# Four feed-forward stages: one 512-column product for a weight's high part in place of two of 256 columns, with the halves summed on VectorE

## The chip, the cores and the metric

The kernel runs on one core of one Trainium2 chip. The metric is the device time of one execution in microseconds (us), as the median of several runs; lower is better.

## The reference, cut to what matters

Two blocks are applied to one sequence of 256 positions with 1024 channels, all in float32. The first has a gated mixer, a SwiGLU feed-forward stage, a banded attention and another SwiGLU stage. The second has, twice, a mixer (convolution, block attention and gated linear attention) and a feed-forward stage with a causal convolution of three taps between the two matrix products. So there are four feed-forward stages (FFN), two without taps and two with:

```python
def _swiglu_ffn(x, g_norm, w_gate_up, w_down):
    h = _rms_norm(x, g_norm)
    gate, up = jnp.split(h @ w_gate_up, 2, axis=-1)
    return (jax.nn.silu(gate) * up) @ w_down
...
        u = causal_depthwise_conv(h @ ffn_w_up[l].astype(h.dtype), ffn_conv_w[l], ffn_conv_b[l])
        x = x + (jax.nn.silu(u[..., :D_FF]) * u[..., D_FF:]) @ ffn_w_down[l].astype(x.dtype)
```

The hidden width is 2816 in all four, which is 22 blocks of 128.

## The kernel before

**Split products.** TensorE multiplies in fp32r, a rounded float32. To keep float32 accuracy every operand is split into a high part, which is the value rounded to fp32r, and a low part, which is the remainder. A product of two split operands is three products on TensorE: high by high, high by low and low by high.

**The weight stream** (class `Stream`). SyncE loads weights in units of two tiles of 128x1024 into three `raw` buffers. ScalarE writes the high part of a tile (`_hi`, L105, "hi" below), and VectorE the low part (`_lo`, L116, "lo" below). `LOOK = 8` pairs of such tiles (`wh`, `wl`) are kept, so the split runs up to eight tiles ahead of TensorE, and `pump` issues the next hi and lo between other work. Four of the down weights of each FFN are split early into buffers of their own (`xh`, `xl`).

**An FFN stage** (`ffn`). The activations stand transposed in SBUF as `hT`, channels on partitions, 256 positions as columns, eight blocks `k` of 128 channels, in two tiles for high and low. The first two of the 22 blocks of the hidden width are computed in another layout (`mmA`). For each block `i` from 2 to 21, a "pair" below, `mmB2` computes the gate and the up projection with two weight tiles. `mmB` runs three products of 256 columns for each `k` (L350 to L352), eight `k`, so a pair is 48 products. They fill one PSUM bank with 256 columns of gate and 256 of up. `finish` makes the activation of the pair: Silu on ScalarE (L628), a multiplication on VectorE (L629), and the split into `ah` and `al` (`split2`, L232 on ScalarE and L233 on VectorE). In the two stages with taps it first applies them: bias and last tap on ScalarE (L617), the two other taps on VectorE (L622, four instructions), all reading PSUM.

Behind the pair, `down` (L374 to L376) multiplies the activation of three pairs ago by its down weight into four accumulators `acc` of 512 columns, 12 products of 512 columns for a pair: two halves `t` of 128 positions, two halves of the 1024 output channels, three products each. At the end of a stage the last activations are needed at once. `boundary` then adds the accumulators to the stream `x`, normalises it, and transposes it into the next `hT`, while `down` for the second half of the positions (`tail`) keeps TensorE at work.

**PSUM.** There are eight banks in one pool. Four hold `acc` during most of an FFN stage, and four are left for the pairs, of which each takes one.

**Order.** SyncE's queue is in program order. The order of the other engines' instructions is set when the program is built, by a scheduler that knows program order and its own costs.

Of the kernel before, what the change touches and what calls it, by code (L numbers as in the profile page):

```python
# [8 lines left out]
F32 = mybir.dt.float32  # L9
F32R = mybir.dt.float32r  # L10
U32 = mybir.dt.uint32
AF = mybir.ActivationFunctionType
# [3 lines left out]
P = 128  # L16
S = 256
D = 1024
KD = D // P
# [28 lines left out]
class Stream:  # L48
# [3 lines left out]
    def __init__(self, nc, raw_pool, pool, units):  # L52
        self.nc, self.raw_pool, self.pool = nc, raw_pool, pool
        self.units = units
        self.raw = {}
        self.split = {}
        self.index = []
        for u, (src, ext) in enumerate(units):
            for j, e in enumerate(ext):
                self.index.append((u, j, j == len(ext) - 1, e))  # L60
        self.next_dma = 0
        self.nh = 0
        self.nl = 0
        self.used = 0
        self.order = [[i for i, p in enumerate(self.index) if p[3] == e] for e in (False, True)]
        self.ext_pool = None
        self.ext_left = 0
        self.row_gain = {}
# [82 lines left out]
class Net:  # L151
    def __init__(self, ctx, tc, a, out, units):
        self.tc, self.nc, self.a, self.out = tc, tc.nc, a, out
        nc = self.nc
        en = ctx.enter_context
        self.cst = en(tc.tile_pool(name="cst", bufs=1))


        self.cst.tile([P, 32], F32, name="pad")
        self.raw_pool = en(tc.tile_pool(name="raw", bufs=RAW))  # L160
        self.wpool = en(tc.tile_pool(name="w", bufs=LOOK))
        self.hpool = en(tc.tile_pool(name="h", bufs=4))
        self.work = en(tc.tile_pool(name="work", bufs=2))
        self.small = en(tc.tile_pool(name="small", bufs=8))
        self.small.tile([P, 48], F32, tag="pad", name="pad", bufs=1)
        self.psum = en(tc.tile_pool(name="psum", bufs=8, space=bass.MemoryType.PSUM))
        en(tc.manual_schedule(engines={mybir.EngineType.SP}))
        self.ws = Stream(nc, self.raw_pool, self.wpool, units)
        self.x = [self.cst.tile([P, D], F32, name=f"x{t}") for t in range(2)]
        self.acc = None  # L170
        self.own = {}
# [13 lines left out]
    def mm(self, shape, name="mm"):  # L185
        return self.psum.tile(shape, F32, tag="mm", name=name, bufs=8)
# [37 lines left out]
        return y  # L224

    def new_hT(self):
        return tuple(
            self.hpool.tile([P, KD, S], F32R, tag="hT", name=n) for n in ("hTh", "hTl")
        )

    def split2(self, hi, lo, src):
        self.nc.scalar.activation(hi, src, AF.Copy)  # L232
# [111 lines left out]
    def mmB(self, out, hT, w):  # L344

        mm = self.nc.tensor.matmul
        vh = w[0].rearrange("p (k n) -> p k n", n=P)
        vl = w[1].rearrange("p (k n) -> p k n", n=P)
        for k in range(KD):
            mm(out, lhsT=vh[:, k, :], rhs=hT[0][:, k, :], start=(k == 0), stop=False)  # L350
            mm(out, lhsT=vh[:, k, :], rhs=hT[1][:, k, :], start=False, stop=False)  # L351
            mm(out, lhsT=vl[:, k, :], rhs=hT[0][:, k, :], start=False, stop=(k == KD - 1))  # L352

    def mmB2(self, hT, name="mm"):

        ids, ws = self.ws.take(2)
        ps = self.mm([P, 2, S], name)
        for j in range(2):
            self.mmB(ps[:, j, :], hT, ws[j])
        self.ws.release(ids)  # L360
        return ps
# [239 lines left out]
    def ffn(self, hT, fin, next_gains, conv=None, final=False):  # L601
        nc = self.nc
        with self.tc.tile_pool(name="ff", bufs=1) as pool:
            self.ws.ext(pool, DEFER)
            acts = {}

            def finish(i, ps):

                if conv is None:
                    g, u = ps[:, 0, :], ps[:, 1, :]  # L610
                else:
                    gu = pool.tile([P, 2, S], F32, tag="gu", name="gu", bufs=2)
                    ws3 = []
                    for j in range(2):
                        q = C_FCV + (conv * 44 + j * NPAIR + i) * 4
                        w = [self.prm[:, q + n : q + n + 1] for n in range(4)]
                        nc.scalar.activation(gu[:, j, :], ps[:, j, :], AF.Identity,  # L617
                                             bias=w[3], scale=w[2])
                        ws3.append(w)
                    for d in (1, 2):  # L620
                        for j in range(2):
                            nc.vector.scalar_tensor_tensor(  # L622
                                gu[:, j, d:], ps[:, j, : S - d], ws3[j][2 - d], gu[:, j, d:],
                                op0=ALU.mult, op1=ALU.add,
                            )
                    g, u = gu[:, 0, :], gu[:, 1, :]
                sg = pool.tile([P, S], F32, tag="sg", name="sg", bufs=2)
                nc.scalar.activation(sg, g, AF.Silu)  # L628
                nc.vector.tensor_mul(sg, sg, u)  # L629
                act = tuple(  # L630
                    pool.tile([P, S], F32R, tag=n, name=n, bufs=7) for n in ("ah", "al")
                )
                self.split2(act[0], act[1], sg)
                acts[i] = act

            ids, ws = self.ws.take(4)
            raws = []
            for t in range(2):
                ps = self.mm([P, 512])
                self.mmA(ps, hT, t, ws, 512, 2, fin if t == 0 else None)  # L640
                gr = self.work.tile([P, 512], F32, tag="hn", name="gr", bufs=2)
                nc.scalar.activation(gr[:, :256], ps[:, :256], AF.Copy)
                nc.vector.tensor_copy(gr[:, 256:], ps[:, 256:])
                raws.append(gr)
                self.ws.pump(2)
            self.ws.release(ids)
            self.ws.pump(2)
            held = []
            for i in range(2, NPAIR):
                ps = self.mmB2(hT)  # L650
                if i == 2:
                    for pr in range(2):
                        pt = self.mm([P, 2, S], "tr")
                        for t in range(2):
                            for j in range(2):
                                c = (j * 2 + pr) * P
                                nc.tensor.transpose(pt[:, j, t * P : (t + 1) * P],
                                                    raws[t][:, c : c + P], self.ident)
                        finish(pr, pt)
                if i < NPAIR - 1:  # L660
                    self.ws.pump(2)
                finish(i, ps)
                if i == 3:
                    self.new_acc()
                if i == 12:
                    gs = [self.gain(g) for g in next_gains]
                d = i - 3
                if d < 0:
                    continue
                ids, ws = self.ws.take(1, d >= NPAIR - DEFER)  # L670
                part = [(acts[d], ws[0])]
                self.down(0, part, d == 0, False)
                if d < NPAIR - DEFER:
                    self.down(1, part, d == 0, conv == 1 and d == NPAIR - DEFER - 1)
                    self.ws.release(ids)
                else:
                    held.append((ids, part[0]))
                if i < NPAIR - 1:
                    self.ws.pump(2)
            for ds in ((NPAIR - 3,), (NPAIR - 2, NPAIR - 1)):  # L680
                ids, ws = self.ws.take(len(ds), True)
                parts = [(acts[d], w) for d, w in zip(ds, ws)]
                self.down(0, parts, False, len(ds) == 2)
                held += [([i], p) for i, p in zip(ids, parts)]

            def tail(mid=None, cuts=(0, 512, 1024)):
                self.down(1, [p for _, p in held], conv == 1, True, mid, cuts)
                for ids, _ in held:
                    self.ws.release(ids)
                self.ws.ext(None, 0)  # L690

            if final:
                return self.boundary([gs[1]], tail, gs[0])
            if conv == 1:
                return gs, tail
            return self.boundary(gs, tail)
# [768 lines left out]
```

## Time and profile before

| what | value |
|---|---|
| median of 3 runs | 1251.49 us (1251.44 to 1251.61) |
| the profiled execution: time, span from first to last instruction | 1251.51 us, 1249.7 us |
| TensorE busy | 1239.1 us, 99% |
| VectorE busy, ScalarE busy | 847.9 us (68%), 666.2 us (53%) |
| granted clock of TensorE, mean | 0.999 of 2.4 GHz |

Durations in the trace are those of single instructions. Products on TensorE overlap one another, so what one costs is read from start to start and not from its duration. ScalarE's and VectorE's instructions overlap their neighbours by some 0.07 to 0.1 us. "PEld" is the loading of weights into the array, which goes on beside the products. A bracket at the end of a row of the timeline gives the idle time ahead of the instruction and what ended it.

### The profile page before, as it was taken

To read this page: it belongs to the slowest core of one execution; us is meant where nothing else is said; L and a number is where in the kernel's file an instruction comes from. 1 tells how busy PE (TensorE), PEld (TensorE's weight loads), DVE (VectorE), ACT (ScalarE), POOL (GpSimd) and SP (SyncE) were. 2 spreads that over 40 slices of the span, in tenths; PEclk is the share of its full clock that TensorE was granted. 3 is DMA by queue.
4 is the path that set the end of the run, shared out by engine and by line. 5 is a ranking of instruction groups with operands and counts; after the bars stand their busy time and mean duration, and the time that the engine had idled before them with its cause. 6 is when DMAs were issued, how large, how long until landed. Compare 5 with 4: busy or idle time off the path is not lost.

```text
span 1249.7 us, 20742 instructions
## 1 busy us (share of the span) xinstructions
PE 1239.1 (99%) x8440; PEld 1122.3 (90%) x8440; DVE 847.9 (68%) x1337; ACT 666.2 (53%) x1077; POOL 40.1 (3%) x95
## 2 busy tenths in 40 slices
PE   8999999999999999999999999999999999999997
PEld 7899899999888889999989878999998978999997
DVE  6676565555567756565568867777775977868764
ACT  7644454544456545454446556556553745656542
POOL 1100000000000000000010010000001011000000
PEclk9999999999999999999999999999999999999999
DMA  7754465665444435566524345456542415555710
GB/s 286 305 200 169 152 217 188 217 255 185 153 165 165 160 136 202 184 235 242 183 103 169 118 162 193 173 200 257 197 169 82 168 74 219 203 195 210 250 71 34
DMA packets 34836, 226.29 MB, mean 181 GB/s; under 512 B 4243, under 2 KB 4661, under 8 KB 9141
## 3 DMA queue, kind: packets, MB, share of 16 engines
q1 hardware_dynamic: 34596, 224.97, 49.2%
q8 instruction: 66, 1.08, 0.3%
q14 instruction: 30, 0.24, 0.1%
q10 hardware_dynamic: 144, 0.00, 0.0%
HBM read 223.91 MB, written 1.05 MB: 180 GB/s over the span
## 4 chain that ended last, share of the span: by engine, by line
PE 97%; DVE 1%; ACT 1%; DMA 0%; POOL 0%; issue 0%; POOLq 0%; ACTq 0%
PE mm L350 17%; PE mm L351 17%; PE mm L352 17%; PE mm L339 12%; PE acc L374 9%; PE acc L375 9%; PE acc L376 9%; PE tr L239 1%; PE sc L709 1%; PE mm L478 1%; PE pt L740 1%; PE sp L559 1%; PE po L798 1%; ACT sq L196 0%; PE po L1165 0%; PE dS L1053 0%
## 5 line engine op out<-in xcount | busy, mean ns | idle before, releaser
L116 DVE TENSOR_TENSOR wl<-raw,wh 128x1024 fp32r<-128x1024 f32 x378 | 458.4, 1223 | 253.2 <-ACT wh L105 250.4
L105 ACT ACTIVATE wh<-raw 128x1024 fp32r<-128x1024 f32 x378 | 394.7, 1055 | 321.6 <-PE mm L351 220.3
L350 PE MATMUL mm<-hTh,wh 128*128 128x256 f32 x1728 | 491.0, 284 | 0.0
L351 PE MATMUL mm<-hTl,wh 128*128 128x256 f32 x1728 | 489.0, 283 | 0.1
L352 PE MATMUL mm<-hTh,wl 128*128 128x256 f32 x1728 | 488.8, 283 | 0.0
L350 PEld LDWEIGHTS mm<-hTh,wh 128*128 128x128 f32 x1728 | 331.1, 192 | 8.4 <-issue 5.2
L351 PEld LDWEIGHTS mm<-hTl,wh 128*128 128x128 f32 x1728 | 331.2, 192 | 3.7 <-DVE hTl L233 0.5
L352 PEld LDWEIGHTS mm<-hTh,wl 128*128 128x128 f32 x1728 | 331.2, 192 | 0.0
L374 PE MATMUL acc<-wh,ah 128*128 128x512 f32 x320 | 126.0, 394 | 0.0
L375 PE MATMUL acc<-wl,ah 128*128 128x512 f32 x320 | 125.4, 392 | 0.0
L376 PE MATMUL acc<-wh,al 128*128 128x512 f32 x320 | 124.5, 389 | 0.0
L339 PE MATMUL mm<-wl,hTh 128*128 128x512 f32 (+1 forms) x240 | 90.2, 381 | 0.0
L339 PE MATMUL mm<-wh,hTh 128*128 128x512 f32 (+1 forms) x240 | 90.1, 381 | 0.0
L232 ACT ACTIVATE ah<-sg 128x256 fp32r<-128x256 f32 x88 | 36.3, 415 | 84.0 <-DVE sg L629 84.0
L622 DVE SCALAR_TENSOR_TENSOR gu<-mm,prm,gu 128x255 f32<-128x255 f32 (+1 forms) x160 | 66.5, 476 | 13.8 <-ACT gu L617 13.6
L376 PEld LDWEIGHTS acc<-wh,al 128*128 128x128 f32 x320 | 60.1, 188 | 13.2
L374 PEld LDWEIGHTS acc<-wh,ah 128*128 128x128 f32 x320 | 60.4, 189 | 10.8 <-issue 0.3
L375 PEld LDWEIGHTS acc<-wl,ah 128*128 128x128 f32 x320 | 60.4, 189 | 9.5
L339 PE MATMUL mm<-wh,hTl 128*128 128x512 f32 (+1 forms) x240 | 61.5, 384 | 0.0
L233 DVE TENSOR_TENSOR al<-sg,ah 128x256 fp32r<-128x256 f32 x88 | 37.1, 424 | 30.1 <-ACT ah L232 30.1
L339 PEld LDWEIGHTS mm<-wl,hTh 128*128 128x128 f32 x240 | 45.1, 188 | 9.3 <-issue 1.1
L339 PEld LDWEIGHTS mm<-wh,hTh 128*128 128x128 f32 x240 | 45.1, 188 | 9.0 <-issue 0.7
(217 smaller groups left out, 1252.0 us busy)
## 6 DMA issues: line engine op xcount, KB each, us to landing
raw<-in_w_ffn SPq DMA_DIRECT2D x66, 1024.0 KB, 4.8
raw<-in_w_up SPq DMA_DIRECT2D x66, 1024.0 KB, 5.0
raw<-in_w_mix SPq DMA_DIRECT2D x30, 1024.0 KB, 4.7
raw<-in_w_gmlp SPq DMA_DIRECT2D x22, 1024.0 KB, 4.8
raw<-in_w_att SPq DMA_DIRECT2D x16, 1024.0 KB, 4.8
raw<-in_w_gmlp SPq DMA_DIRECT2D x4, 512.0 KB, 6.3
bias<-in_rel SPq DMA_DIRECT2D x8, 256.0 KB, 3.9
x<-in_x SPq DMA_DIRECT2D x4, 256.0 KB, 5.4
```

Source lines behind the costliest of these rows:

```text
L105: self.nc.scalar.activation(hi, r, AF.Copy, scale=1.0 if g is None else g)
L116: self.nc.vector.tensor_sub(lo, r, hi.bitcast(F32))
L232: self.nc.scalar.activation(hi, src, AF.Copy)
L233: self.nc.vector.tensor_sub(lo, src, hi.bitcast(F32))
L339: mm(out, lhsT=hT[a][:, k, ts], rhs=view(b, k), start=(i == 0), stop=(i == 3 * KD - 1))
L350: mm(out, lhsT=vh[:, k, :], rhs=hT[0][:, k, :], start=(k == 0), stop=False)
L351: mm(out, lhsT=vh[:, k, :], rhs=hT[1][:, k, :], start=False, stop=False)
L352: mm(out, lhsT=vl[:, k, :], rhs=hT[0][:, k, :], start=False, stop=(k == KD - 1))
L374: mm(acc, lhsT=act[0][:, ts], rhs=w[0][:, c], start=(first and i == 0), stop=False)
L375: mm(acc, lhsT=act[0][:, ts], rhs=w[1][:, c], start=False, stop=False)
L376: mm(acc, lhsT=act[1][:, ts], rhs=w[0][:, c], start=False, stop=(last and i == n - 1))
L622: nc.vector.scalar_tensor_tensor(gu[:, j, d:], ps[:, j, : S - d], ws3[j][2 - d], gu[:, j, d:], op0=ALU.mult, op1=ALU.add,)
```

## The change

In `ffn` the high part of a weight tile now meets both parts of the activations in one product of 512 columns (`wide`), and its low part meets the high activations in one of 256 columns (`low`). For this the high and the low activations of a `k` lie side by side in one tile (`new_hT`). The wide product leaves high by high in the first 256 columns of a PSUM bank and high by low in the second 256, and the low product is added into the first half. So gate and up need a bank each, and `finish` has to add the two halves of each: ScalarE copies the second half out of PSUM and VectorE adds the first to it, into a tile `sum` in SBUF. What follows (Silu or the taps) reads `sum`. In the stages with taps, Silu is done in place. The other users of `mmB` are not changed.

```diff
     def new_hT(self):
-        return tuple(
-            self.hpool.tile([P, KD, S], F32R, tag="hT", name=n) for n in ("hTh", "hTl")
-        )
+        t = self.hpool.tile([P, KD, 2, S], F32R, tag="hT", name="hT")
+        return t[:, :, 0, :], t[:, :, 1, :], t
...
+    def mmB_wide(self, hT, w):
+        mm = self.nc.tensor.matmul
+        ps = self.mm([P, 2, S])
+        vh = w[0].rearrange("p (k n) -> p k n", n=P)
+        vl = w[1].rearrange("p (k n) -> p k n", n=P)
+        def wide(k):
+            mm(ps, lhsT=vh[:, k, :], rhs=hT[2][:, k], start=(k == 0), stop=(k == KD - 1))
+        def low(k):
+            mm(ps[:, 0, :], lhsT=vl[:, k, :], rhs=hT[0][:, k, :], start=False, stop=False)
+        for k in range(KD):
+            for f in (wide, low) if k < KD - 1 else (low, wide):
+                f(k)
+        return ps
...
             def finish(i, ps):
+                if isinstance(ps, list):
+                    raw = pool.tile([P, 2, S], F32, tag="sum", name="sum", bufs=2)
+                    for j in range(2):
+                        nc.scalar.activation(raw[:, j, :], ps[j][:, 1, :], AF.Copy)
+                    for j in range(2):
+                        nc.vector.tensor_add(raw[:, j, :], ps[j][:, 0, :], raw[:, j, :])
+                    ps = raw
...
-                sg = pool.tile([P, S], F32, tag="sg", name="sg", bufs=2)
+                if conv is None:
+                    sg = pool.tile([P, S], F32, tag="sg", name="sg", bufs=2)
+                else:
+                    sg = g
...
             for i in range(2, NPAIR):
-                ps = self.mmB2(hT)
+                if wide:
+                    ids, ws = self.ws.take(2)
+                    ps = [self.mmB_wide(hT, w) for w in ws]
+                    self.ws.release(ids)
+                else:
+                    ps = self.mmB2(hT)
```

## Rows read from the trace of the kernel before

**Rows 1.** The page, part 1: busy time, share of the span, instructions.
```profile
PE 1239.1 (99%) x8440; PEld 1122.3 (90%) x8440; DVE 847.9 (68%) x1337; ACT 666.2 (53%) x1077; POOL 40.1 (3%) x95
```

**Rows 2.** The page, part 4: the chain that ended last, by engine.
```profile
PE 97%; DVE 1%; ACT 1%; DMA 0%; POOL 0%; issue 0%; POOLq 0%; ACTq 0%
```

**Rows 3.** Groups of instructions: products of the changed loops and of others.
```profile
L350 PE MATMUL mm<-hTh,wh 128*128 128x256 f32 x1728 | 491.0, 284 | 0.0
```

**Rows 4.** The timeline of TensorE over one pair and its down products (start, duration).
```profile
799.48 0.28 PE L350 MATMUL mm<-hTh,wh 128*128 128x256 f32 x1
...
805.23 0.40 PE L374 MATMUL acc<-wh,ah 128*128 128x512 f32 x1
...
807.98 0.28 PE L350 MATMUL mm<-hTh,wh 128*128 128x256 f32 x1
```

**Rows 5.** The chain in order of time: start, length, what, count.
```profile
354.42 10.90 PE mm L339 x48
...
664.33 11.50 PE mm L339 x72
```

**Rows 6.** Groups by shape, and single lines (minimum/median/maximum in ns): 256-column work.
```profile
L642 ACT ACTIVATE gr<-mm x8: 364/371/380, 159.3 to 1067.4; 128x256 f32<-128x256 f32 x8
...
L629 DVE TENSOR_TENSOR sg<-sg,mm x40: 413/415/416, 176.4 to 635.9; 128x256 f32<-128x256 f32 x40
...
L617 ACT ACTIVATE gu<-mm,prm x80: 546/552/567, 778.4 to 1232.6; 128x256 f32<-128x256 f32 x80
...
L932 ACT ACTIVATE cy<-hpad,prm x4: 601/602/603, 661.3 to 966.3; 128x256 f32<-128x256 f32 x4
...
L622 DVE SCALAR_TENSOR_TENSOR gu<-mm,prm,gu 128x255 f32<-128x255 f32 x80 | 35.0, 477 | 13.8 <-ACT gu L617 13.6
...
L921 DVE SCALAR_TENSOR_TENSOR cy<-hpad,prm,cy 128x256 f32<-128x256 f32 x120 | 51.2, 478 | 1.6 <-ACT cy L932 1.3
```

**Rows 7.** The timeline of VectorE over one pair of a stage with taps.
```profile
899.91 1.23 DVE L116 TENSOR_TENSOR wl<-raw,wh 128x1024 fp32r<-128x1024 f32 x1 [1.41 <-ACT wh L105]
901.05 1.65 DVE L622 SCALAR_TENSOR_TENSOR gu<-mm,prm,gu 128x255 f32<-128x255 f32 x4
902.77 1.23 DVE L116 TENSOR_TENSOR wl<-raw,wh 128x1024 fp32r<-128x1024 f32 x1
903.92 0.42 DVE L629 TENSOR_TENSOR sg<-sg,gu 128x256 f32<-128x256 f32 x1
904.82 0.43 DVE L233 TENSOR_TENSOR al<-sg,ah 128x256 fp32r<-128x256 f32 x1 [0.48 <-ACT ah L232]
905.77 1.23 DVE L116 TENSOR_TENSOR wl<-raw,wh 128x1024 fp32r<-128x1024 f32 x1 [0.52 <-ACT wh L105]
```

**Rows 8.** The timeline of ScalarE in the same pair: what its hi waited for.
```profile
901.68 1.06 ACT L105 ACTIVATE wh<-raw 128x1024 fp32r<-128x1024 f32 x1 [0.90 <-PE acc L376]
```

**Rows 9.** Timelines at the end of the first FFN stage: TensorE, ScalarE, VectorE.
```profile
329.69 0.40 PE L374 MATMUL acc<-xh,ah 128*128 128x512 f32 x1
...
333.12 0.39 PE L374 MATMUL acc<-xh,ah 128*128 128x512 f32 x1
...
329.83 1.06 ACT L105 ACTIVATE wh<-raw 128x1024 fp32r<-128x1024 f32 x1 [1.88 <-PE mm L351]
330.79 0.37 ACT L628 ACTIVATE sg<-mm 128x256 f32<-128x256 f32 x1
332.51 0.42 ACT L232 ACTIVATE ah<-sg 128x256 fp32r<-128x256 f32 x1 [1.35 <-DVE sg L629]
...
330.92 1.23 DVE L116 TENSOR_TENSOR wl<-raw,wh 128x1024 fp32r<-128x1024 f32 x1 [1.72 <-ACT wh L105]
332.06 0.41 DVE L629 TENSOR_TENSOR sg<-sg,mm 128x256 f32<-128x256 f32 x1
```

**Rows 10.** Timelines at the end of the third FFN stage: ScalarE, TensorE.
```profile
937.31 0.42 ACT L232 ACTIVATE ah<-sg 128x256 fp32r<-128x256 f32 x1 [0.49 <-DVE sg L629]
...
942.94 0.66 PE L239 MATMUL tr<-ident,hn 128*128 128x128 f32 x4 [0.34 <-DVE hn L221]
```

More of the change, by code (lines that the diff above doesn't have):

```diff
@@ L161, in __init__ @@
         self.wpool = en(tc.tile_pool(name="w", bufs=LOOK))
-        self.hpool = en(tc.tile_pool(name="h", bufs=4))
+        self.hpool = en(tc.tile_pool(name="h", bufs=2))
         self.work = en(tc.tile_pool(name="work", bufs=2))
@@ L605, in ffn @@
             acts = {}
+            wide = True
             def finish(i, ps):
+                if isinstance(ps, list):
[5 more added lines that the diff above has]
+                    ps = raw
                 if conv is None:
```

## The prediction

> **What bounds the kernel now.** I read the page first. TensorE is busy 99% of the span, VectorE 68%, ScalarE 53% [rows 1]. A busy TensorE need not be a fast one, so I went to the chain that ended last: 97% of it is TensorE [rows 2]. Nothing but TensorE's own stream of products sets the time, except in short places between stages, so the question is what one product costs, and whether the other engines keep up when the products get fewer.
>
> The cost of a product is read from start to start. In the timeline a pair begins at 799.48 and its first down product at 805.23: 5.75 us for 48 products of 256 columns, 0.1198 each. The 12 down products of 512 columns last until 807.98: 2.75 us, 0.2292 each [rows 4]. The chain has a stretch of 48 products of 512 columns without a stop, 10.90 us or 0.2271 each, and one of 72, of which 24 have 512 columns and 48 have 272, in 11.50 us: (11.50 - 24 x 0.2271) / 48 = 0.126 for 272 columns [rows 5]. At 2.4 GHz, one column per cycle, 256, 272 and 512 columns are 106.7, 113.3 and 213.3 ns. So each product costs its columns and some 13 ns more (13.1, 12.7 and 13.8), whatever its width. Fewer, wider products with the same columns save 13 ns each.
>
> **The change, part by part.**
>
> *Products.* For each `k` three products of 256 columns become one of 512 and one of 256; the columns stay 768. Before: 3 x 0.1198 = 0.3594. After: 0.2271 + 0.1198 = 0.3469. A pair has 16 such steps: 5.75 becomes 5.55, 0.20 less. The four stages have 20 pairs each. As a check, 4 x 20 x 16 = 1280 of the 1728 instructions of L350 lie in them [rows 3]; the rest is in the mixers and the attention, which keep the old loop. The sum is 80 x 0.20 = 16.0 us saved. With the dearer 0.2292 of the down products for the wide product, a pair saves 0.166 and the whole 13.3. If the wide product cost its columns and the 12.7 ns of the 272-column one, 1.1 ns less, 1280 x 1.1 ns = 1.4 us more would be saved. I take 0.2271, from the longest stretch of such products that nothing interrupts. Each product still has its own weights to be loaded, one load fewer per `k`; the shortest product beside which a load must fit is one of 256 columns, as in every step of today's loop.
>
> The Trainium skill would price it otherwise. "TensorE: Matmul & The Clock Gate", section "Back-to-back issue gap", gives a matmul at full clock N / 2.4 plus about 2.5 ns; by that, an estimate from the page, one product fewer per `k` saves 1280 x 2.5 ns = 3.2 us, not 16. The trace does not agree: 13 ns beyond the columns at three widths.
>
> *The two halves.* Each pair gains two copies of 256 columns from PSUM on ScalarE, at 0.371 (the nearest row is L642, the same copy), and two additions on VectorE with one operand in PSUM, at 0.415 (L629 with `mm`) [rows 6]. Over 80 pairs that is 59 us more for ScalarE and 66 us for VectorE. Both stay far below TensorE over the whole span: 725 and 914 of some 1237. So they cost nothing as long as their order leaves room. The place to look is the stages with taps.
>
> *The taps out of SBUF.* VectorE's tap costs 477 ns out of PSUM (L622), and the same kind of instruction with all operands in SBUF 478 (L921): no gain. ScalarE's tap costs 552 out of PSUM and 602 out of SBUF (L617 and L932): 0.05 more, twice a pair [rows 6]. That is hidden like the copies. Silu in place costs nothing and adds no wait, since the multiplication behind it writes the same place today.
>
> *Does VectorE keep up in a stage with taps?* In one pair of 8.50 us it idles 1.41 + 0.48 + 0.52 = 2.41, so its work takes 6.09 [rows 7]. With two additions, 6.92. The pair shrinks to 5.55 + 2.75 = 8.30, so 1.38 is left for waits. The 1.41 goes away when time is short: it waits for a hi that itself waits for TensorE to free a weight buffer (ScalarE idles 0.90 ahead of one for that reason [rows 8]), which means that the stream runs as far ahead as its buffers allow. The 0.48 and 0.52 follow from the order, multiply, split high, split low, hi, lo, and stay: 1.00. So it fits, with 0.38 to spare. Behind VectorE's additions queue the taps, the split and the next lo; TensorE waits for the first only three pairs later and for the lo only when six tiles of lead are used up.
>
> *PSUM.* A pair takes two of the four free banks, so pair i + 2 needs those of pair i. From the end of pair i that is 2.75 + 5.55 + 2.75 = 11.05 us. The copies and additions are done after about 3.2 us even behind a hi and a lo (the sums in the next part), so some 7.8 us are spare. Cost nothing; without that cover it would be a stall of TensorE at each pair.
>
> *The end of a stage.* Here the cover is gone. In the first stage the last pair ends at 329.69 and TensorE wants the high part of its activation at 333.12, after 15 down products. ScalarE does a hi (329.83) and then Silu (330.79), VectorE a lo (330.92) and then the multiplication (332.06), ScalarE the split (332.51, done 332.93): 0.19 to spare [rows 9]. Now copies and additions come in. Bound below: the first half is ready early, because gate's bank is complete half a pair sooner, and only the second copy and addition come after the pair. The copy starts at 330.79, the addition behind the lo at 332.06, the multiplication at 332.48 in place of 332.06: 0.42 later, of which 0.19 is spare, so 0.25 of stall. Bound above: both copies come behind the hi and both additions behind the lo, then Silu, then the multiplication: 332.06 + 0.8 + 0.4, or 1.17 later, a stall of 0.98. I take 0.6, about midway, since the order is the scheduler's and no row favours an end. The second stage has the same chain: 0.6 too. In the third the split ends at 937.73, later against its pair by the taps; TensorE there fills with products of the second half, and then waits 0.34 for the normalised rows before the transposes at 942.94 [rows 10]: the delay comes through whole, 0.42 to 1.17, taken as 0.8. In the last stage the second half's products stand beside, with nothing due that early: 0. The sum is 2.0 us, with the ends 0.9 and 3.1.
>
> *The sum.* Against the profiled execution's 1251.51, which stands at the median of the runs (1251.49): 1251.5 - 16.0 + 2.0 = 1237.5. Best ends: 1251.5 - 17.4 + 0.9 = 1235.0. Worst: 1251.5 - 13.3 + 3.1 = 1241.3.
>
> **The rivals.**
>
> *Slower: the round trip between ScalarE and VectorE becomes the bound in the stages with taps.* Place: the additions. If the scheduler puts the copies behind a hi and gives VectorE nothing else to do, the addition waits for the hi, 0.96 from its start to the next instruction's [rows 9], and both copies, 0.74; less the 0.38 to spare that is 1.3 too much: a pair of about 9.6 against 8.30. The lead covers the first 7.8 us of such an excess in a stage (the spare time of the PSUM banks); the rest, some 18 steady pairs x 1.3 - 7.8 = 15.6, comes through in each of two stages: 1237.5 + 31 = 1269. It turns the gain of 14.0 into a loss from 2 x (18 x e - 7.8) = 14, an excess e of 0.82 a pair; below 0.43 it costs nothing. For it: work and fixed waits would fill 6.92 + 1.00 = 7.92 of VectorE's 8.30, 95%. Against it: in today's pair the scheduler puts a lo into VectorE's wait for Silu (902.77 in rows 7), so it fills such gaps. Chance of any cost 0.13, of a loss against before 0.07.
>
> *The change saves nothing on TensorE.* That is the case if the 13 ns belong to a column, not to a product: in the wide product, where the moving operand is the activations, it may cost twice the narrow one's 0.1198. Nothing is saved: 1251.5 + 2.0 = 1253.5. With a fifth of the 13 ns saved it would be 1251.5 - 3.3 + 2.0 = 1250.2. (The estimate by "TensorE: Matmul & The Clock Gate" of the Trainium skill, above, would come out there.) For it: no 512-column product of today has activations as its moving operand. Against it: three widths lie on one line. Chance 0.06.
>
> *PSUM runs short at the start of a stage.* Pairs 2 and 3, the two transposed blocks and the four accumulators want ten banks of eight close together, when VectorE has three activations to finish. If TensorE waits there for half of VectorE's work on one activation, (1.65 + 0.42 + 0.43) / 2 or some 1.2 us [rows 7], in each stage, 1237.5 + 4.8 = 1242.3. Chance 0.11.
>
> **How the numbers follow.** The forecast, 1237.5 within 1235.0 to 1241.3, has 0.70; the PSUM rival 0.11; VectorE's round trip 0.13; nothing saved 0.06. Two runs of this kernel can be told apart from about 0.2%, 2.5 us. Faster than that: 0.70 + 0.11 + 0.05 of the round trip = 0.86; the same: 0.01 of it and 0.04 of the third case = 0.05; slower: 0.07 and 0.02 = 0.09. The range goes from a little under the best end, 1234.5, to 1246, which takes in the PSUM rival and the mild half of the round trip; what lies above has 0.15.
>
> **What the profile will show.** Starts of the wide products 0.227 apart from the following narrow ones, and those 0.120 from the next: a pair of 5.55. VectorE's idle time in a pair with taps down from 2.41 to about 1.4, and hi's still waiting for TensorE (if they wait no more, the stream has lost its lead). Between the last pair of stages one to three and the first down product of its activation, a gap on TensorE of 0.3 to 1.2. The prediction is wrong if the wide product takes over 0.235, if TensorE shows waits for VectorE within the pairs, or if the ends of the stages lose over 1.2 us each.

## The result, and the profile after

The changed kernel takes 1240.25 us (median; 1240.22 to 1240.47) where the kernel before took 1251.47 beside it: a ratio of 0.9911, 95% interval 0.9899 to 0.9923. The profiled execution took 1240.27, with a span of 1238.5 at a granted clock of 0.999. So 11.2 us are gone, where 14.0 were forecast, and the sum that led there was right in its direction, wrong in the size of two of its terms, and without a third.

The page of the changed kernel, busy time first, then the chain that ended last, by engine:

```profile
PE 1228.8 (99%) x7160; PEld 1055.0 (85%) x7160; DVE 903.5 (73%) x1497; ACT 715.1 (58%) x1237; POOL 41.3 (3%) x95
...
PE 97%; DVE 2%; ACT 1%; POOL 0%; issue 0%; POOLq 0%; ACTq 0%
```

As before [rows 1, 2], TensorE's stream sets the time: 97% of the chain. It has 1280 products fewer (7160 for 8440). VectorE and ScalarE took on 55.6 and 48.9 us.

The groups of the new instructions, by shape (busy us and mean ns of one, then idle time ahead of them):

```profile
L363 PE MATMUL mm<-hT,wh 128*128 128x512 f32 x1280 | 452.1, 397 | 0.0
...
L366 PE MATMUL mm<-hT,wl 128*128 128x256 f32 x1280 | 333.2, 281 | 0.0
...
L636 DVE TENSOR_TENSOR sum<-mm,sum 128x256 f32<-128x256 f32 x160 | 66.6, 419 | 15.1 <-ACT sum L634 15.0
L634 ACT ACTIVATE sum<-mm 128x256 f32<-128x256 f32 x160 | 58.8, 369 | 31.1 <-PE mm L363 30.7
L646 ACT ACTIVATE gu<-sum,prm 128x256 f32<-128x256 f32 x80 | 46.6, 595 | 21.1 <-DVE sum L636 21.1
...
L651 DVE SCALAR_TENSOR_TENSOR gu<-sum,prm,gu 128x255 f32<-128x255 f32 x80 | 37.4, 478 | 3.6 <-ACT gu L646 3.5
```

The four prices off TensorE are the ones taken from [rows 6]: addition 419 ns (0.415 taken), copy 369 (0.371), ScalarE's tap from SBUF 595 (602), VectorE's 478 (478). The idle time ahead of the two products is nought: nothing holds them up from outside.

What a product costs is read from start to start in TensorE's timeline, one pair and its down products:

```profile
901.37 0.39 PE L363 MATMUL mm<-hT,wh 128*128 128x512 f32 x1
901.60 0.28 PE L366 MATMUL mm<-hT,wl 128*128 128x256 f32 x1
901.71 0.40 PE L363 MATMUL mm<-hT,wh 128*128 128x512 f32 x1
901.95 0.28 PE L366 MATMUL mm<-hT,wl 128*128 128x256 f32 x1
902.06 0.40 PE L363 MATMUL mm<-hT,wh 128*128 128x512 f32 x1
...
907.01 0.40 PE L393 MATMUL acc<-wh,ah 128*128 128x512 f32 x1
...
909.73 0.39 PE L363 MATMUL mm<-hT,wh 128*128 128x512 f32 x1
```

The first wide product takes 0.23, the second, behind a narrow one, 0.24; the two narrow ones take 0.11. The pair takes 907.01 - 901.37 = 5.64, its 12 down products 909.73 - 907.01 = 2.72. Over all 80 pairs the means are 5.635 for a pair, 234.9 ns for a wide product and 117.3 for a narrow one; one `k` costs 352 ns, against 359 before [rows 4] and 347 forecast.

The 2.72 is new as well: it was 2.75 [rows 4]. This is where the kernel before spent the difference, in its TensorE timeline behind the pair of [rows 4], whose first down product starts at 805.23:

```profile
806.39 0.39 PE L376 MATMUL acc<-wh,al 128*128 128x512 f32 x1
...
807.75 0.39 PE L376 MATMUL acc<-wh,al 128*128 128x512 f32 x1
```

The first five down products took (806.39 - 805.23) / 5 = 0.232, the next six (807.75 - 806.39) / 6 = 0.227. So 512 columns cost more just behind a run of 256-column products. In the changed kernel only the first of the twelve is dear, at 0.233, and the other eleven take 0.227: one wide product stands ahead of them. The means over the stages are 2.748 before and 2.727 after.

The balance, summed over the four stages of both traces: the 80 pairs take 450.8 us for 460.5, which is 9.7 less, and what stands between them, the down products above all, 199.5 for 201.0, which is 1.5 less. These two make the 11.2. What else changed nearly cancels: the stretch ahead of the first stage's pairs is 0.6 shorter (163.7 for 164.3), and the stretches behind the last pairs of the four stages change by -0.1, 0.0, +0.1 and +0.4.

VectorE over one pair of a stage with taps (idle time ahead of an instruction, and what ended it, in brackets):

```profile
896.02 0.42 DVE L661 TENSOR_TENSOR gu<-gu 128x256 f32<-128x256 f32 x1
897.12 1.23 DVE L116 TENSOR_TENSOR wl<-raw,wh 128x1024 fp32r<-128x1024 f32 x1 [0.69 <-ACT wh L105]
898.26 0.42 DVE L233 TENSOR_TENSOR al<-gu,ah 128x256 fp32r<-128x256 f32 x1
898.60 0.42 DVE L636 TENSOR_TENSOR sum<-mm,sum 128x256 f32<-128x256 f32 x1
899.94 1.23 DVE L116 TENSOR_TENSOR wl<-raw,wh 128x1024 fp32r<-128x1024 f32 x1 [0.93 <-ACT wh L105]
901.08 0.42 DVE L636 TENSOR_TENSOR sum<-mm,sum 128x256 f32<-128x256 f32 x1
901.42 1.91 DVE L651 SCALAR_TENSOR_TENSOR gu<-sum,prm,gu 128x255 f32<-128x255 f32 x4
903.24 1.22 DVE L116 TENSOR_TENSOR wl<-raw,wh 128x1024 fp32r<-128x1024 f32 x1
```

Its waits in the pair fall from 2.41 [rows 7] to 0.69 + 0.93 = 1.62, and both are for a hi, neither for the split nor for a copy. The order is another one: gate's addition stands two instructions ahead of up's.

The end of the first FFN stage, timelines of TensorE, ScalarE and VectorE:

```profile
326.29 0.40 PE L393 MATMUL acc<-xh,ah 128*128 128x512 f32 x1
...
324.96 0.41 ACT L660 ACTIVATE sg<-sum 128x256 f32<-128x256 f32 x1
326.49 0.38 ACT L634 ACTIVATE sum<-mm 128x256 f32<-128x256 f32 x1 [1.13 <-PE mm L363]
326.77 1.05 ACT L105 ACTIVATE wh<-raw 128x1024 fp32r<-128x1024 f32 x1
327.82 0.42 ACT L232 ACTIVATE ah<-sg 128x256 fp32r<-128x256 f32 x1
...
326.90 0.42 DVE L636 TENSOR_TENSOR sum<-mm,sum 128x256 f32<-128x256 f32 x1 [0.59 <-ACT sum L634]
327.36 0.42 DVE L661 TENSOR_TENSOR sg<-sg,sum 128x256 f32<-128x256 f32 x1
```

Silu has already run at 324.96, before the pair ends at 326.29, because gate's bank was complete half a pair earlier. Only up's copy and addition follow the pair, with the hi behind the copy instead of ahead of it. The multiplication starts 327.36 - 326.29 = 1.07 behind the pair's end, where it was 332.06 - 329.69 = 2.37 [rows 9]. The chain behind the pair got shorter, not longer. TensorE did not wait for it there before either, so it gains almost nothing by it (0.1 us).

In the last stage, for which the prediction put nothing, TensorE does wait for the activation of the last pair, which ends there at 1220.31 (ScalarE's split, then TensorE):

```profile
1223.61 0.42 ACT L232 ACTIVATE ah<-gu 128x256 fp32r<-128x256 f32 x1 [1.53 <-DVE gu L661]
...
1223.48 0.39 PE L395 MATMUL acc<-xh,al 128*128 128x512 f32 x1
1224.08 0.50 PE L393 MATMUL acc<-xh,ah 128*128 128x512 f32 x1 [0.21 <-ACT ah L232]
```

The product starts 0.60 behind the one ahead of it in place of 0.23, and the next one 0.34 behind it: half a microsecond lost. In the kernel before, the products there follow one another at 0.23. The third stage has the same kind of gap, 0.43 and then 0.34, where the kernel before had 0.26 and 0.34.

### The profile page after: what moved, and what is told of

Read it like the earlier page. It is cut to its first block, busy times and chain, and to the rows that moved or that the text cites. A ratio compares the mean times of both kernels' runs of the same rounds, so it can differ in the third digit from the quotient of the medians.

```text
span 1238.5 us, 18456 instructions
## 1 busy us (share of the span) xinstructions
PE 1228.8 (99%) x7160; PEld 1055.0 (85%) x7160; DVE 903.5 (73%) x1497; ACT 715.1 (58%) x1237; POOL 41.3 (3%) x95
## 4 chain that ended last, share of the span: by engine, by line
PE 97%; DVE 2%; ACT 1%; POOL 0%; issue 0%; POOLq 0%; ACTq 0%
PE mm L363 24%; PE mm L339 12%; PE mm L366 12%; PE acc L393 9%; PE acc L395 9%; PE acc L394 9%; PE mm L350 5%; PE mm L351 4%; PE mm L352 4%; PE tr L239 1%; PE sc L746 1%; PE mm L497 1%; PE pt L777 1%; PE sp L578 1%; PE po L835 1%; PE po L1202 0%
## 5 line engine op out<-in xcount | busy, mean ns | idle before, releaser
L116 DVE TENSOR_TENSOR wl<-raw,wh 128x1024 fp32r<-128x1024 f32 x378 | 458.8, 1223 | 201.0 <-ACT wh L105 200.1
L363 PE MATMUL mm<-hT,wh 128*128 128x512 f32 x1280 | 452.1, 397 | 0.0
L366 PE MATMUL mm<-hT,wl 128*128 128x256 f32 x1280 | 333.2, 281 | 0.0
L363 PEld LDWEIGHTS mm<-hT,wh 128*128 128x128 f32 x1280 | 235.2, 188 | 46.2
L366 PEld LDWEIGHTS mm<-hT,wl 128*128 128x128 f32 x1280 | 241.6, 189 | 14.2
L339 PE MATMUL mm<-wh,hT 128*128 128x512 f32 (+1 forms) x480 | 149.1, 383 | 0.0
L350 PE MATMUL mm<-hT,wh 128*128 128x256 f32 x448 | 128.9, 288 | 0.0
L351 PE MATMUL mm<-hT,wh 128*128 128x256 f32 x448 | 126.8, 283 | 0.1
L352 PE MATMUL mm<-hT,wl 128*128 128x256 f32 x448 | 126.6, 283 | 0.0
L339 PEld LDWEIGHTS mm<-wh,hT 128*128 128x128 f32 x480 | 86.8, 188 | 16.8 <-issue 1.1
L350 PEld LDWEIGHTS mm<-hT,wh 128*128 128x128 f32 x448 | 85.7, 191 | 5.5 <-issue 5.2
L339 PE MATMUL mm<-wl,hT 128*128 128x512 f32 (+1 forms) x240 | 90.2, 381 | 0.0
L351 PEld LDWEIGHTS mm<-hT,wh 128*128 128x128 f32 x448 | 85.8, 192 | 0.7 <-DVE hT L233 0.5
L352 PEld LDWEIGHTS mm<-hT,wl 128*128 128x128 f32 x448 | 85.8, 191 | 0.0
L636 DVE TENSOR_TENSOR sum<-mm,sum 128x256 f32<-128x256 f32 x160 | 66.6, 419 | 15.1 <-ACT sum L634 15.0
L651 DVE SCALAR_TENSOR_TENSOR gu<-sum,prm,gu 128x255 f32<-128x255 f32 (+1 forms) x160 | 72.7, 480 | 5.4 <-ACT gu L646 3.5
```

What stands on the lines that cost most here:

```text
L116: self.nc.vector.tensor_sub(lo, r, hi.bitcast(F32))
L339: mm(out, lhsT=hT[a][:, k, ts], rhs=view(b, k), start=(i == 0), stop=(i == 3 * KD - 1))
L363: mm(ps, lhsT=vh[:, k, :], rhs=hT[2][:, k], start=(k == 0), stop=(k == KD - 1))
L366: mm(ps[:, 0, :], lhsT=vl[:, k, :], rhs=hT[0][:, k, :], start=False, stop=False)
L651: nc.vector.scalar_tensor_tensor(gu[:, j, d:], ps[:, j, : S - d], ws3[j][2 - d], gu[:, j, d:], op0=ALU.mult, op1=ALU.add,)
```

## The experiments

Three theories stood for the dear wide product (235 ns for the forecast 227). A: it is dear because it stands behind a narrow one, that is, TensorE loses time where the width changes. B: it is dear in itself, through its moving operand, 512 columns of activations in two parts. C: it is dear because the product ahead writes half of the same PSUM bank. Beside that: what the copies and additions cost, and how far the round trip of ScalarE and VectorE is from being the bound.

**grouped**: the products of a tile in three runs, so that the width changes less often.

```diff
+        wide(0)
         for k in range(KD):
-            for f in (wide, low) if k < KD - 1 else (low, wide):
-                f(k)
+            low(k)
+        for k in range(1, KD):
+            wide(k)
```

> Of a weight tile's 16 products, the order is one wide, the eight narrow, then seven wide, in place of wide and narrow by turns. Theory A, the alternation costs: a wide product takes 0.235 us from start to start only beside narrow ones, and 0.227 among its like; narrow ones take 0.120 among theirs. Then a pair takes 16 x 0.347 = 5.55 in place of 5.635, and the time is 1240.25 - 80 x 0.085 = 1233.5 us; if the first wide products after a run of narrow ones are dearer, as the first down products after a pair were before (0.234, 0.235, 0.229, 0.232, 0.231), up to 0.028 a tile comes back, 1238. Theory B, the operand: with activations as the moving operand a wide product takes 0.235 in any order; 1240 within 1. Theory C, the bank: each product adds into the bank that the one before has just written, which here stays so; 1240 within 1.

Measured: 1236.17 (1236.12 to 1236.26), ratio 0.9878 (0.9864 to 0.9893); a pair takes 5.591. Its TensorE timeline, equal products in one row:

```profile
891.32 2.00 PE L363 MATMUL mm<-hT,wh 128*128 128x512 f32 x8
893.16 1.12 PE L366 MATMUL mm<-hT,wl 128*128 128x256 f32 x8
894.11 1.78 PE L363 MATMUL mm<-hT,wh 128*128 128x512 f32 x7
895.73 0.39 PE L395 MATMUL acc<-wh,ah 128*128 128x512 f32 x1
```

Eight narrow products take 0.95, 0.119 each; the seven wide ones behind them 1.62, 0.231 each. One by one these seven take 233, 236, 228, 233, 231, 227 and 227 ns. The same wide products on the same operands and banks reach 227 once the run of narrow ones is five products back: B is refuted, A holds, with something that A had not said, that the return to 512 columns costs several products a little each.

**two_banks**: wide and narrow alternate as in the change, but each narrow product belongs to the other tile, and so writes another bank than the wide ones beside it.

```diff
+        wide(0, 0)
+        for k in range(KD - 1):
+            wide(1, k)
+            low(0, k)
+        low(0, KD - 1)
+        for k in range(1, KD):
+            wide(0, k)
+            low(1, k - 1)
+        low(1, KD - 1)
+        wide(1, KD - 1)
```

> Wide and narrow products alternate as in the changed kernel, but neighbours belong to the two weight tiles of the pair, so each product writes another PSUM bank than the one before it. Theory C, the bank: wide 0.227 and narrow 0.117 or less, a pair of 5.5, about 1231 us. Theories A (alternation) and B (operand): wide 0.235 and narrow 0.117 as before, 1240 us; gate's bank is now complete only at the end of the pair, which may cost up to 1 us at the ends of the stages, 1241.

Measured: 1243.71 (1243.66 to 1244.21), ratio 0.9939 (0.9925 to 0.9954). A pair takes 5.637, a wide product 235.2 and a narrow one 117.1 ns, as in the change (5.635, 234.9, 117.3). The bank makes no difference: C falls. The kernel is nevertheless 3.5 us slower than the changed one, at the same pair. VectorE at the end of the first stage, where the first down product starts at 326.56:

```profile
326.76 0.43 DVE L660 TENSOR_TENSOR sum<-mm,sum 128x256 f32<-128x256 f32 x1 [2.07 <-ACT sum L658]
...
328.86 0.42 DVE L660 TENSOR_TENSOR sum<-mm,sum 128x256 f32<-128x256 f32 x1
329.24 1.23 DVE L116 TENSOR_TENSOR wl<-raw,wh 128x1024 fp32r<-128x1024 f32 x1
330.38 0.42 DVE L685 TENSOR_TENSOR sg<-sg,sum 128x256 f32<-128x256 f32 x1
```

The multiplication comes 330.38 - 326.56 = 3.82 behind the pair's end, not 1.07. With the tiles interlaced, gate's bank is complete only just ahead of up's, and both additions, with a lo between each two steps, follow the pair. Of the 3.5 us, 2.6 lie behind the last pairs of the first three stages (0.8, 1.3 and 0.5), and most of the rest in the down products, which take 2.738 in place of 2.727. That is about the size of the bad stage end of the prediction's upper bound (0.98, 0.98 and 1.17): it exists, in another order of the products.

**sums_narrow**: the sums without the wide product. The three products of 256 columns stay, but they go into two halves of a tile's bank, which are copied and added as in the change.

```diff
+        for k in range(KD):
+            mm(ps[:, 0, :], lhsT=vh[:, k, :], rhs=hT[0][:, k, :], start=(k == 0), stop=False)
+            mm(ps[:, 0, :], lhsT=vl[:, k, :], rhs=hT[0][:, k, :], start=False, stop=(k == KD - 1))
+        for k in range(KD):
+            mm(ps[:, 1, :], lhsT=vh[:, k, :], rhs=hT[1][:, k, :], start=(k == 0), stop=(k == KD - 1))
```

> The products of the kernel before, 24 narrow ones for a weight tile, but written into the two halves of a bank for each tile and summed as in the changed kernel: the sums and the two banks alone. TensorE's pair should be 5.75 again. If the sums cost nothing, 1251.5 us within 1; if they cost what the prediction took for the ends of the stages, 1253.5; if the order that the scheduler finds with gate's bank ready early helps, below 1251.

Measured: 1252.12 (1251.97 to 1252.33), ratio 1.0006 (0.9996 to 1.0015). By the medians the copies and additions by themselves cost 0.7 us; the interval runs from 0.5 us of gain to 1.9 of cost, so it includes none at all. A pair takes 5.757, as before (5.756). All of the gain is the wide product's. The first down product behind the narrow ones takes 233 ns again.

**no_sums**: the changed kernel without copies and additions. The second half of each bank, high weights by the low part of the activations, is left out of the result.

```diff
-                if isinstance(ps, list):
...
-                    ps = raw
+                pj = [ps[j][:, 0, :] if isinstance(ps, list) else ps[:, j, :] for j in range(2)]
```

> The changed kernel without the copies and additions: what follows reads the first half of each bank, so the product of the high weights with the low activations is computed and left out of the result in these stages. If the sums cost nothing, 1240.3 us within 0.7. If they cost 2.0 us at the ends of the stages as predicted, 1238.2. If VectorE holds TensorE up anywhere in a pair, more than that, 1236 or below.

Measured: 1239.29 (1239.21 to 1239.33), ratio 0.9903 (0.9888 to 0.9918). That is 12.1 us under the kernel before measured beside it, where the changed kernel was 11.2 under: 0.9 us apart. In the traces 0.8 and 0.5 of it lie behind the last pairs of the two stages with taps; behind that of the first stage 0.3 is lost, and the pairs take the same 5.635. The 0.60 and 0.34 at the end of the last stage are gone: those products follow at 0.227. In sums_narrow the gap is there (0.52 and 0.34). So the sums cost about 1 us, where 2.0 were put down to them. In the last stage it is TensorE's wait for the last activation; in the third that is 0.2 of the 0.8, and the rest was not followed.

**one_switch**: over both tiles of a pair, all narrow products in one run, with gate's bank still complete before up's.

```diff
+        for k in range(KD):
+            wide(0, k)
+        wide(1, 0)
+        for j in range(2):
+            for k in range(KD):
+                low(j, k)
+        for k in range(1, KD):
+            wide(1, k)
```

> The order over the whole pair: gate's eight wide products, up's first wide one, the eight narrow ones of gate, the eight of up, up's other wide ones. TensorE goes from narrow to wide once in a pair, not twice as in the grouped order. If each such return costs what it did there, 2.805 - 8 x 0.2267 - 8 x 0.120 = 0.02 to 0.03 us less what the first narrow ones give back, a pair takes 5.57 in place of 5.59 and the time is 1236.2 - 1.6 = 1234.6 us. If the cost goes with the number of narrow products, the pair stays at 5.59 and the time at 1236.2. Gate's bank is complete 0.2 us later than in the grouped order, which should not show.

Measured: 1235.08 (1234.59 to 1235.22), ratio 0.9869 (0.9855 to 0.9884), the fastest here. TensorE's timeline over a pair:

```profile
889.07 2.20 PE L380 MATMUL mm<-hT,wh 128*128 128x512 f32 x9
891.11 2.08 PE L383 MATMUL mm<-hT,wl 128*128 128x256 f32 x16
893.02 1.78 PE L380 MATMUL mm<-hT,wh 128*128 128x512 f32 x7
894.64 0.39 PE L415 MATMUL acc<-wh,ah 128*128 128x512 f32 x1
```

Nine wide products behind down products of the same width take 2.04, 0.2267 each; 16 narrow ones 1.91, 0.1194 each; the seven behind them 0.2314 each, as behind eight narrow ones. The loss is that of the return, and a run of 16 in place of eight hardly makes it larger.

**runs_of_two**: two wide, two narrow, and so on.

```diff
+        for k in range(0, KD - 2, 2):
+            for f in (wide, low):
+                f(k)
+                f(k + 1)
+        wide(KD - 2)
+        low(KD - 2)
+        low(KD - 1)
+        wide(KD - 1)
```

> Two wide, two narrow, and so on. There are four returns from narrow to wide in a weight tile in place of eight. If a return costs 7 ns whatever the length of the run, a pair takes 5.635 - 8 x 0.007 = 5.58, the time 1235.8 us. If it grows with the run (14 ns for two), the pair stays at 5.635 and the time at 1240.3.

Measured: 1238.99 (1238.68 to 1240.82), ratio 0.99 (0.9884 to 0.9917); a pair takes 5.607, between the two values expected. With the price of products among their own kind, 16 x (0.2271 + 0.1198) = 5.550 for a pair and the 2.720 that 12 down products take in grouped and one_switch, the orders compare like this. The down products stand in the table because a return close to the end of a pair is paid in part by them:

| Order | Returns to 512 columns in a pair | Narrow ones ahead of each | Pair, us | Down products, us | Above 5.550 + 2.720, per return |
|---|---|---|---|---|---|
| changed kernel | 14 | 1 (2 at a tile's end) | 5.635 | 2.727 | 7 ns |
| two_banks | 14 | 1 (2 at two places) | 5.637 | 2.738 | 8 ns |
| runs_of_two | 8 | 2 | 5.607 | 2.738 | 9 ns |
| grouped | 2 | 8 | 5.591 | 2.720 | 20 ns |
| one_switch | 1 | 16 | 5.572 | 2.720 | 21 ns |
| kernel before, pair into down products | 1 | 48 | 5.756 | 2.748 | 28 ns (down products alone, above 2.720) |

A return costs 7 to 8 ns behind one narrow product, 9 behind two and 20 to 21 behind eight or more: it grows with the run, but less than in proportion, and behind eight hardly any more. Fewer returns win in every order.

**no_low**: the narrow products left out (low part of the weights missing from the result), so that TensorE has as little to do in a pair that ScalarE and VectorE show how fast they can go.

```diff
         for k in range(KD):
-            for f in (wide, low) if k < KD - 1 else (low, wide):
-                f(k)
+            wide(k)
```

> The narrow products are left out, so the low part of the weights is not multiplied in these stages; all else stays. It measures how long the other engines need for a pair, which the changed kernel hides. TensorE alone would need 16 x 0.227 + 2.72 = 6.35 us for a pair, wide products being among their like at 0.227. If VectorE and ScalarE need the 6.92 + 1.00 = 7.9 of the prediction in the stages with taps and less than 6.35 in the others, pairs settle at 7.9 and 6.35, and the time is near 1240 - 40 x 2.0 - 40 x 0.45 = 1142, less some 15 for the lead: about 1127 us. If they keep up everywhere, 1080. If they need over 8.3, the changed kernel lives on its lead, and the time is over 1145.

Measured: 1099.38 (1098.97 to 1099.79), ratio 0.8785 (0.8768 to 0.8803). Wide products among themselves take 227 ns. A pair with its down products takes 6.35 in the stages without taps; in those with taps 6.35 at first, 6.5 to 7.9 in the pairs in which VectorE has an extra lo, and about 6.6 later. VectorE over one such pair:

```profile
791.18 0.42 DVE L233 TENSOR_TENSOR al<-gu,ah 128x256 fp32r<-128x256 f32 x1 [0.22 <-ACT ah L232]
791.53 0.75 DVE L635 TENSOR_TENSOR sum<-mm,sum 128x256 f32<-128x256 f32 x2
792.19 1.22 DVE L116 TENSOR_TENSOR wl<-raw,wh 128x1024 fp32r<-128x1024 f32 x1
793.33 1.66 DVE L650 SCALAR_TENSOR_TENSOR gu<-sum,prm,gu 128x255 f32<-128x255 f32 x4
794.90 1.22 DVE L116 TENSOR_TENSOR wl<-raw,wh 128x1024 fp32r<-128x1024 f32 x1
796.04 0.42 DVE L660 TENSOR_TENSOR gu<-gu 128x256 f32<-128x256 f32 x1
796.37 1.22 DVE L116 TENSOR_TENSOR wl<-raw,wh 128x1024 fp32r<-128x1024 f32 x1
797.51 0.42 DVE L233 TENSOR_TENSOR al<-gu,ah 128x256 fp32r<-128x256 f32 x1
```

From split to split 6.33, three lo's, two additions and the taps included, and no wait but 0.22 in front. When VectorE is short of time, its waits go: the scheduler's order has something else to do in each. It does not keep up quite everywhere: the stretch behind the third stage's last pair takes 142.1 us, where the changed kernel takes 134.0. What of this is a lead of the weight stream that was used up was not followed.

**medium**: is it short products that cost, or any change of width? The low part of the weights meets 384 columns instead of 256 (the extra 128 go into the second half: the product of low by low, which the kernel leaves out, for half of the positions).

```diff
-            mm(ps[:, 0, :], lhsT=vl[:, k, :], rhs=hT[0][:, k, :], start=False, stop=False)
+            mm(ps.rearrange("p a s -> p (a s)")[:, 0:384], lhsT=vl[:, k, :],
+               rhs=hT[2][:, k].rearrange("p a s -> p (a s)")[:, 0:384], start=False, stop=False)
```

> Wide and narrow alternate as in the changed kernel, but the low weights meet 384 columns: the high activations and the first 128 of the low ones, a term that the reference's float32 has and the changed kernel drops. If any change of width costs, a wide and a medium product take 0.227 + 0.160 + 0.013 + 0.007 = 0.407 us together, a pair 6.51, and the time is 1240.3 + 80 x 0.88 = 1311 us. If only products as short as 256 columns leave something that the next wide one pays back, 0.400 together, a pair 6.40, and 1301.

Measured: 1314.83, ratio 1.0507 (1.0476 to 1.0537); a pair takes 6.542. TensorE's timeline:

```profile
899.74 0.40 PE L363 MATMUL mm<-hT,wh 128*128 128x512 f32 x1
899.97 0.34 PE L366 MATMUL mm<-hT,wl 128*128 128x384 f32 x1
900.15 0.39 PE L363 MATMUL mm<-hT,wh 128*128 128x512 f32 x1
900.38 0.34 PE L366 MATMUL mm<-hT,wl 128*128 128x384 f32 x1
```

512 and 384 columns at 227.1 and, with the same 13 ns, 173 would be 400 together. They take 406.5 in gate's tile (231 to 232 and 175) and 413 in up's (237 and 176). So alternating costs at 384 columns too, 6.5 to 13 ns for each two products. Why up's tile loses twice as much as gate's is open.

## Why the prediction came out as it did

*Products: the mechanism right, the size wrong.* The forecast was 5.55 for a pair, 16.0 us saved in all; 5.635 and 9.7 us came, less than the term's low end of 13.3. The step that failed is "each product costs its columns and some 13 ns more, whatever its width". It holds among products of one width: 227 and 119 to 120 in every run above. It does not hold for a 512-column product behind a 256-column one, and the change puts one there 14 times in a pair. Per `k` the wide product lost 7.8 ns on 227.1 and the narrow one gained 2.5 on 119.8, which takes 5.3 ns of the forecast 12.5. The sign was in [rows 4, 5], and I read past it: the down products cost 0.2292 in the one and products of that width 0.2271 in the other. I took these as two prices of one thing and chose the lower. They were the same price plus the cost of a return, which the first five of the twelve paid. The second stretch of [rows 5] has it too: its 24 products of 512 columns stand behind those of 272 and take 228.3 on the mean, the first six 234, 235, 225, 230, 236 and 229, so 272 columns cost 125.4 and not 126. The limit named in the prediction, a wide product over 0.235, was almost reached: its mean is 234.9 ns.

*Down products: a term left out.* They were taken as unchanged. With a wide product ahead, each pair saves 0.021 on them, 1.5 us in all. It is the same effect with the opposite sign.

*The Trainium skill's price.* "TensorE: Matmul & The Clock Gate", section "Back-to-back issue gap", has N / 2.4 plus about 2.5 ns as the gap of an isolated matmul, and says that against a stream of weight loads and matmuls it counts too little at small N and too much at large N; the prediction left that out. No run agrees with the formula: 227 is 13.7 ns above 512 columns, 119.4 is 12.7 above 256, so for the wide ones too it counts too little, not too much. The 3.2 us estimated by it compare with 9.7 here and 80 x (5.756 - 5.572) = 14.7 in one_switch.

*Ends of the stages: 2.0 forecast, 0.5 came, and in another place.* Of the two ends given for the first stage even the lower, a multiplication 0.42 later, was too dark: it is 1.30 earlier. I had seen that gate's bank is complete half a pair sooner, but gave credit for one copy and addition alone. Silu moved ahead of the pair's end with them, and the order put up's copy ahead of the hi. That the early bank does it is shown by two_banks, where it is missing and 2.6 us are lost at the ends. So the first three stages lost nothing on the whole. The last stage, put at 0 because nothing would be due that early, lost 0.4: TensorE there wants the activation of the last pair after 15 down products, as in the first stage, and waits.

*The total: near by luck.* The products fell 6.3 us short. Against that stand the 1.5 of the down products, the 1.5 too much for the ends, and 0.6 ahead of the first stage that nothing here explains. These errors of opposite sign almost cancel, so the forecast of 1237.5 missed by 2.8 us where its largest term missed by 6.3.

*Sums and taps: hidden, as forecast, but for about 1 us.* The 0.7 of sums_narrow and the 0.9 of no_sums agree. The cost lies at the ends of the two stages with taps, where the split of the last activation comes behind an addition and the taps; all of it in the last stage, and a part in the third, is TensorE's wait for that split.

*VectorE in a stage with taps: it fits, by more than I said.* I counted 6.92 of work and 1.00 of waits that stay, 7.92 of 8.30. The waits do not stay: no_low shows a pair in 6.33 with 0.22 of waiting, and in the changed kernel the wait for the split is gone and only the two for a hi are left. A wait that another instruction could fill is not a cost of the order. So the rival of the round trip, a pair of 9.6, was further off than its 0.13: of the changed kernel's 8.36 for a pair and its down products the 6.55 of no_low's later pairs leave some 1.8 us of cover, not 0.38.

*The other rivals.* "Nothing saved" falls with sums_narrow and the change: same sums, 11.9 us apart. PSUM short at a stage's start: in the changed kernel's waits TensorE waits for VectorE for a weight's lo (0.8 us, twice, at L497, outside these stages), for the normalised rows (0.3) and once for an activation's high part (the 0.21 of the last stage, where gaps of 0.3 to 1.2 in the first three were expected), nowhere for a bank; the eight banks were enough.

## What to carry to other kernels

Price a product from a stretch where it has the neighbours it will have: two prices for one shape in one trace are a question, and here the answer, what stands ahead of it, was worth 6.3 us. Let products of equal width stand together and change width seldom: one_switch has the products of the change, in another order, and takes 1235.1 us in place of 1240.25. And when results are to be summed off TensorE at the end of a stage, have the first of two banks complete early; interlacing the two cost 2.6 us there.

## What the runs showed of the hardware

A change from 256 to 512 columns costs TensorE time that no wait in the profile shows. Behind a long run of narrow products the next wide ones took 233, 236, 228, 233 and 231 ns before they came back to 227, and the first narrow one behind wide ones took 113 where later ones took 120. It does not depend on the bank (two_banks) and the wide operand alone doesn't bring it (no_low); 384 columns beside 512 show it too.

A change of width is enough for it but not needed. Behind the wait at the end of the last stage of the changed kernel all products have 512 columns, and from the second on they took 233, 234, 235, 229, 232 and 231 ns before they came back to 227. So it may be that a run of wide products builds up something that narrow ones use up and a standstill takes away; no run shows what it is: weight loads and the supply of the moving operand were not tried apart. Other orders of the products in the stages that keep the old loop were not tried either.
